# GLA gate, second half: five pairs by seven products, sixteen stored units; PLE preparation, LN1 border and the PLE gate's last units in another order

## The chip, the cores and the metric

The kernel runs on one core of one Trainium2 chip, in one launch. The metric is device time in microseconds. Before the change three runs gave a median of 1651.93 us (1651.26 to 1652.1). One execution was profiled; the trace's rows are from it.

## The reference, cut to what matters

A decoder block over x of 256 tokens by 2048 channels, one layer, all in float32. The part in which the change adds products is the GLA branch's output gate `gr`, one of the column blocks of the combined input projection; two other parts that it reorders are the first layer norm and the per-layer embedding (PLE).

```python
def token_mixers(x, w_in, ...):
    proj = x @ w_in
    gq, gk, gv, gr, glr, fq, fk, fv, ff, ma, mb = jnp.split(proj, offsets, axis=-1)
    ...
    o = gla_chunked(q, k, v, log_a)
    o = o * lax.rsqrt(jnp.mean(o * o, -1, keepdims=True) + RMS_EPS) * gla_norm_g
    o = o.reshape(B, S, GLA_V) * jax.nn.silu(gr)
    y_gla = o @ w_branch_gla
    ...
    merged = jax.nn.sigmoid(ma) * y_gla + jax.nn.sigmoid(mb) * y_fox
    return merged @ w_out

def reference(x, p, ...):
    mix = token_mixers(x, ...)
    x = layer_norm(ALPHA * x + mix, ln1_g, ln1_b)
    ffn = conv_gated_mlp(x, w_gate, w_up, conv_w, conv_b, w_down)
    x = layer_norm(ALPHA * x + ffn, ln2_g, ln2_b)
    return x + jax.nn.sigmoid(x @ w_ple_gate) * (p[0] @ w_ple_proj)
```

## The kernel before

**Units.** All weights come as units of 128 x 2048 float32 (1 MB). `prep()` loads a unit over SP's queue in two halves of 512 KB into `raw` (a ring of five buffers), ACT copies each half to `hi` in the rounded type fp32r (L121), and DVE subtracts to get the remainder `lo` (L241). A product of an activation and a weight is made of three matmuls: activation hi by weight hi, hi by lo, lo by hi. `unit()` gives the next unit to PE's code and prepares up to three ahead.

**Halves.** `s_half` (L818) makes a 2048-deep projection for 1024 output columns: eight pairs of 128-deep blocks, one unit each, into four PSUM quadrants (two of tokens, two of columns) of 128 x 512. A *classic* pair takes 24 matmuls of 512 columns (L844). A pair listed in the half's `_S` table goes by Strassen's seven products instead, 21 matmuls (L852); it needs sums of activations (`x_sums` for the input projection) and four differences of the unit's quarters (L159, DVE). For the pairs listed in a `_T` table the unit is *stored* (`parked`): `park_gen` loads it early, makes its four differences then, and stores 1 MB to `td` in DRAM over POOL's queue (L172); in the half `prep_s` loads a quarter, a half and the 1 MB of `td`, and DVE only makes the remainders (L215), 512 columns and three times 1024. A pair in `_S` but not in `_T` loads the plain unit and makes the differences within the half. After the last Strassen pair `fold` (L862) adds the products' PSUM tiles into the output tile.

**The stored units of the input projection** are those of the two `gv` and two `gr` halves. `park_gen` steps through them in three lots: the first four during FoX, the next four during the GLA's q and k, the rest in the loop of the 20 merge-gate units (`for n in range(PSM1)`), in which PE also makes the chunk scores `pa` (L735) from DVE's `kq` tiles (L718) and DVE makes `x_sums`.

**Order.** A scheduler orders each engine by priorities and modelled readiness, except where the code says `manual_schedule` or `keep_in_program_order`. The LN1 border `end1` (L1310) is under manual schedule on PE. There `turn0(g)` and `turn1(g)` transpose group g of the normalized first or second token half (tile `ptl`, L1212), and `proj(k, t)` makes six matmuls `pp` of the PLE projection (L353). `G` is (1, 0, 3, 2). DVE normalizes the groups by L1196 and L1202 and makes `x1T` from the transposed tiles (L1110, L1227); `put(t)` stores `pp`.

**PLE.** `ple_prep(0)` loads two `praw` halves and `pTr`, and makes `pw` (L1275) and `pTs` (L1280) on ACT and DVE. It is called within `out_proj(0, ...)`, the first half `wo` of the output projection, behind a pair named by its index in the order (0, 1, 3, 4, 5, 2, 6, 7); there pairs 1, 2, 3 and 5 are Strassen, all stored.

**The end.** The last half is `pg`, the PLE gate's second half, with pairs 2, 3 and 4 Strassen. Its last `tail` units are run quadrant by quadrant (L893): for each quadrant all its products, then `ev_g` (L1614), which adds PSUM to `zg`, takes a tanh on ACT, and makes `tho` (L1582) and `res` (L1584) on DVE, which SP stores to the output. The quadrant (1,1) comes last, in two halves of 256 columns (`pg_11b`, `pg_11c`, L909); `pre_g` adds what it had before the tail.

Of the kernel before, what the change touches and what calls it, by code (L numbers as in the profile page):

```python
# [49 lines left out]
GV_ORDER = ((0, 1, 2, 3, 4, 5, 7, 6),) * 2  # L50
GV_S = ((1, 2, 4, 5, 7),) * 2
GV_T = ((1, 2, 5, 7), (1, 2, 5, 7))
GR_T = ((1, 2, 5, 7), (2, 5, 7))
GR_S = ((1, 2, 4, 5, 7), (1, 2, 5, 7))
X_S = (1, 2, 4, 5, 7)
WO_S = ((1, 2, 3, 5), (1, 3, 5))
WO_C = (0, 4, 6, 7)
# [9 lines left out]
PG_S = ((), (2, 3, 4))  # L67
# [11 lines left out]
def tile_block(ctx: ExitStack, tc: tile.TileContext, wu, wfv, wpp, xT_in, x_in, pT_in, wlr,  # L79
# [25 lines left out]
    def s8(shape, dt=F32, name=None):  # L105
        return big.tile(shape, dt, tag="S8", name=name)
# [4 lines left out]
    def t2(name):  # L111
        return sm.tile([P, 512], F32, tag="t2", bufs=6, name=name)

    def mmtile(name):
        return pmm.tile([P, 512], F32, tag="mm", name=name)
# [4 lines left out]
    def copy(o, i, scale=1.0):  # L120
        return nc.scalar.activation(o, i, AF.Copy, bias=0.0, scale=scale)  # L121
# [8 lines left out]
    for _ in range(8):  # L130
# [6 lines left out]
    s_units = {b + nh * len(order[nh]) + i  # L137
               for b, order, sset in ((52, GV_ORDER, GV_S), (68, GV_ORDER, GR_S),
                                      (120, OUT_ORDER, WO_S), (dn0, DN_ORDER, DN_S),
# [4 lines left out]
    parked = {b + nh * len(order[nh]) + order[nh].index(n): None  # L144
              for b, order, tset in ((52, GV_ORDER, GV_T), (68, GV_ORDER, GR_T), (120, OUT_ORDER, WO_T),
                                     (dn0, DN_ORDER, DN_T), (NU - 16, PG_ORDER, PG_T))
# [102 lines left out]
    def unit(ahead=3):  # L249
        u = n_used[0]  # L250
        n_used[0] += 1
        while n_prep[0] < min(NU, u + ahead):
            prep()
        return ready.pop(u)
# [532 lines left out]
    def cell(o, i):  # L787

        return o[:, i, 0:P], o[:, i, P:256]
# [230 lines left out]
    for nh in range(2):  # L1020
        def ev_v(t, c, ps, nh=nh):
            z = vg[2 * nh + c][:, 0, t, :]
            with tc.high_priority(P_STAT):
# [3 lines left out]
               residual=False)  # L1027
# [7 lines left out]
    for nh in range(2):  # L1035
        def ev_r(t, c, ps, nh=nh):
# [3 lines left out]
            if 2 * nh + c == 0:  # L1040
                gate(z, z)

        s_half("gr", nh, GV_ORDER[nh], GR_S[nh], x_cl, x_st, lambda t, g: vg[g][:, 1, t, :], ev_r,
               residual=False)
# [187 lines left out]
    def out_proj(nh, tail, mid, end=None):  # L1232
        def cl(pair, j, t):
            if pair not in WO_C:
                return cell(mS[pair], ((0, 7), (1, 2))[j][t])
            i = WO_C.index(pair)
            a = mC[i // 2][:, i % 2 * 2 + j, :]
            return a[:, t * P:t * P + P], a[:, 256 + t * P:256 + t * P + P]

        def ev(t, c, ps):  # L1240
            zc = z1of(t, 2 * nh + c)
            with tc.high_priority(P_STAT):
                nc.vector.tensor_tensor(zc, zc, ps, ALU.add)
                if tail:
                    nc.vector.bn_stats(st1[t][:, 2 * nh + c, :], zc)

        s_half("wo", nh, OUT_ORDER[nh], WO_S[nh], cl, lambda pair, i: cell(mS[pair], i), z1of, ev,
               tail, mid, end)
# [11 lines left out]
    def load_gain(li, i):  # L1260
        g = s8([P, 2048], name=f"lnb{li}{i}")
        nc.sync.dma_start(g, lng[2 * li + i].broadcast_to([P, 2048]))
        gain[li].append(g)

    def ple_prep(half):

        w = [s8([P, 2048], F32R, name=f"pw{half}{i}") for i in range(2)]
        pt_ = s8([P, 2, 512], F32R, name=f"pTs{half}")
        pTs = [pt_[:, k, :] for k in range(2)]
        for k in range(2):  # L1270
            raw = ring.tile([P, 1024], F32, tag="raw", bufs=5, name=f"praw{half}{k}")
            nc.sync.dma_start(raw, wpp[half, :, k * 1024:k * 1024 + 1024])
            o = slice(k * 1024, k * 1024 + 1024)
            copy(w[0][:, o], raw)
            nc.vector.tensor_tensor(w[1][:, o], raw, w[0][:, o].bitcast(F32), ALU.subtract)  # L1275
        pT = t2("pTr").rearrange("p (k t) -> p k t", t=S)
        nc.sync.dma_start(pT, pT_in)
        for k in range(2):
            copy(pTs[k][:, 0:256], pT[:, k, :])
            nc.vector.tensor_tensor(pTs[k][:, 256:512], pT[:, k, :],  # L1280
                                    pTs[k][:, 0:256].bitcast(F32), ALU.subtract)
        return w, pTs
# [12 lines left out]
    def z1of(t, g):  # L1295
        return z1[t][:, g * 512:g * 512 + 512]
# [11 lines left out]
    pq, first = [], []  # L1308

    def end1(tail_mm):  # L1310

        x1T.extend(s8([P, 4, 512], F32R, name=f"x1T{g}") for g in range(4))
        with tc.manual_schedule(engines={mybir.EngineType.PE}):
            pb = [[[mmtile(f"pp0{t}{c}")] for c in range(2)] for t in range(2)]
            ps, us = [], []

            def proj(k, t):
                o = slice(k * 1024, k * 1024 + 1024)  # L1320
                w, pTs = pq[0]
                x_mm(pb, (w[0][:, o], w[1][:, o]), pTs[k], (t,), k == 0, k == 1)

            def put(t):
                for c in range(2):
                    o = t2("ppo")
                    tc.keep_in_program_order(copy(o, pb[t][c][0]))
                    nc.gpsimd.dma_start(ppd[t, :, c * 512:c * 512 + 512], o)

            kts = [4 * g + i for g in LN_ORDER for i in range(4)]  # L1330

            def phase0(i, part):
                if i == len(us):
                    us.append(unit())
                    ps.append(mmtile(("psg0", "psu0", "psg1")[i]))
                w_phase(ps[i], *us[i], x1T, 0, kts, part)

            def phase1(j):
                for i in range(3):
                    w_phase(ps[i], *us[i], x1T, 1, kts, slice(4 * j, 4 * j + 4))  # L1340

            for c in range(2):
                for i in range(2):
                    tail_mm(0, c, i)
            G = LN_ORDER
            (stat0, norm0, turn0), (stat1, norm1, turn1) = [
                ln_steps(z1of, st1, t, x1T, gain[0], c_g1, c_b1, "l1", P_LN1[t], AFF1[t])
                for t in range(2)]
            stat0()
            for g in G[:2]:  # L1350
                norm0(g)
            for i in range(2):
                tail_mm(1, 0, i)
            tail_mm(1, 1, 0)
            turn0(G[0])
            tail_mm(1, 1, 1)
            turn0(G[1])
            stat1()
            for g in G[2:]:
                norm0(g)  # L1360
            proj(0, 0)
            turn0(G[2])
            proj(1, 0)
            proj(0, 1)
            turn0(G[3])
            put(0)
            for g in G[:2]:
                norm1(g)
            proj(1, 1)
            for i in range(3):  # L1370
                phase0(i, slice(0, 12))
                turn1(G[i])
                if i == 0:
                    put(1)
                    for g in G[2:]:
                        norm1(g)
            for i in range(3):
                phase0(i, slice(12, 16))
            for j in range(4):
                phase1(j)  # L1380
                if j == 1:
                    turn1(G[3])
            first.extend(ps)

    def begin_out():
        for pair in (6, 7):
            turn_pair(pair)
        load_z1()

    out_proj(0, 0, {0: begin_out, 3: lambda: pq.append(ple_prep(0)),  # L1390
                    5: lambda: load_gain(0, 0)})
    out_proj(1, 2, {3: lambda: load_gain(0, 1), 4: stats1}, end1)
    mixers.append(affine(z1of, gain[0], lambda t: nc.gpsimd.dma_start(x1d[t], z1[t]), AFF1))
# [78 lines left out]
    pb, pq = [], []  # L1472
# [122 lines left out]
    def g_sums(pairs):  # L1595
        two = s8([P, 8, 256], F32R, name=f"gS{pairs[0]}")
        for i, pair in enumerate(pairs):
            o = two[:, 4 * i:4 * i + 4]
            a = x2T[pair // 2][:, pair % 2 * 2:pair % 2 * 2 + 2, :].bitcast(F32)
            y = t2("gy").rearrange("p (k t) -> p k t", t=S)  # L1600
            nc.vector.tensor_tensor(y, a[:, :, 0:256], a[:, :, 256:512], ALU.add)
            v = s_sums(y)
            copy(o[:, :, 0:P], v)
            nc.vector.tensor_tensor(o[:, :, P:256], v, o[:, :, 0:P].bitcast(F32), ALU.subtract)
            gS_[pair] = o
# [25 lines left out]
    def mid4():  # L1631
# [4 lines left out]
           begin=begin2, mid=(mid4, 4))  # L1636

    s_half("pg", 1, PG_ORDER[1], PG_S[1], g_cl, g_st, lambda t, g: zg[:, t, g - 2, :], ev_g,
           2, {0: lambda: g_sums(PG_S[1][2:])}, residual=False, fine=pre_g)
    assert n_used[0] == NU, (n_used[0], NU)  # L1640


# [46 lines left out]
def _layout(i):  # L1689
# [8 lines left out]
        [np.stack([_wst(c("fq", 1024)), _wst(c("fk", 1024))], 1).reshape(16, P, 2048), qk.reshape(16, P, 2048), m[:PSM1],  # L1698
         _sst(c("gv", 2048), GV_ORDER, GV_S), _sst(c("gr", 2048), GV_ORDER, GR_S), m[PSM1:]] + br
        + [_sst(i["w_out"][0], OUT_ORDER, WO_S), gu,  # L1700
# [45 lines left out]
```

## Time and profile before

| | us |
|---|---|
| median of three runs | 1651.93 |
| the profiled execution | 1650.91 |
| its span, first to last instruction | 1648.4 |
| PE busy | 1639.4 |
| DVE busy | 1336.8 |
| ACT busy | 903.3 |

In the rows shown below, a row of a timeline gives start and duration in us, the engine, the line, the operation, output and inputs, their shapes and a count; a bracket at its end gives the engine's idle time before it and what ended it. A row of the chain gives start, duration, engine, tile, line and count. A row of the windows gives for a stretch its length and each engine's busy time with the number of instructions, the granted clock of TensorE, the share of DMA time and GB/s. Durations of single matmuls overlap; the spacing of two starts tells how fast they go.

### The profile page before, as it was taken

The page shows a single profiled execution, that of the slowest core. Times are in us where ns is not written, and L with a number is a line of the kernel's source. Part 1 is how long each engine was busy: PE and PEld are TensorE (multiplying, and loading weights), DVE is VectorE, ACT ScalarE, POOL GpSimd, SP SyncE. Part 2 cuts the span into 40 slices and gives each one's busy share as a digit, 9 for nine tenths or more (in the row PEclk, how much of TensorE's full clock was granted, in tenths as well). Part 3 has the DMA queues.
Part 4 walks back from the last instruction along what each step waited for, and adds up shares of the span by engine and source line. Part 5 has one row for each costly group of instructions (what it writes and reads, how often), then busy time and mean ns, then how long its engine had stood idle before and what let it go on. Part 6 is the DMA issues. An engine that isn't in the chain of part 4 may idle for free.

```text
span 1648.4 us, 23392 instructions
## 1 busy us (share of the span) xinstructions
PE 1639.4 (99%) x8429; PEld 1405.7 (85%) x8429; DVE 1336.8 (81%) x1920; ACT 903.3 (55%) x1259; POOL 89.3 (5%) x237
## 2 busy tenths in 40 slices
PE   9999999999999999999999999999999999999998
PEld 8988888888888888888888888888888888888887
DVE  7677789888888767778977888888887778989787
ACT  6755545456656654446574454555455456566554
POOL 0000000000000000000010111110111000000000
PEclk9999999999999999999999999999999999999999
DMA  9777689977878658888855898888776679899574
GB/s 324 279 262 277 227 327 343 345 251 281 292 249 283 228 194 313 304 313 308 303 185 190 315 344 319 298 301 309 277 245 216 212 260 344 299 352 341 172 261 152
DMA packets 111669, 457.35 MB, mean 277 GB/s; under 512 B 12681, under 2 KB 13969, under 8 KB 94657
## 3 DMA queue, kind: packets, MB, share of 16 engines
q1 hardware_dynamic: 103056, 404.47, 69.9%
q0 software_dynamic: 8496, 51.39, 8.0%
q8 instruction: 66, 1.08, 0.3%
q14 instruction: 51, 0.41, 0.1%
HBM read 404.42 MB, written 51.39 MB: 277 GB/s over the span
## 4 chain that ended last, share of the span: by engine, by line
PE 98%; DVE 1%; DMA 0%; ACT 0%; issue 0%; POOL 0%; SPq 0%
PE psm L973 11%; PE dn L841 10%; PE psu L307 10%; PE psg L307 9%; PE psa L973 5%; PE psu L309 5%; PE psg L309 5%; PE dn_p L841 4%; PE wo L841 3%; PE gr L841 3%; PE gv L841 3%; PE pg L353 3%; PE psb L973 3%; PE fv L472 3%; PE pg L841 2%; PE psk L307 2%
## 5 line engine op out<-in xcount | busy, mean ns | idle before, releaser
L241 DVE TENSOR_TENSOR lo<-raw,hi 128x1024 fp32r<-128x1024 f32 x466 | 564.6, 1221 | 165.6 <-ACT hi L121 163.5
L121 ACT ACTIVATE hi<-raw 128x1024 fp32r<-128x1024 f32 x466 | 488.8, 1058 | 350.4 <-DMA raw<-in_wu_dram 66.3
L307 PE MATMUL psu<-x1T,hi 128*128 128x512 f32 x688 | 240.4, 392 | 0.0
L307 PE MATMUL psg<-x1T,hi 128*128 128x512 f32 x672 | 234.9, 392 | 0.0
L309 PE MATMUL psu<-x1T,lo 128*128 128x256 f32 x688 | 192.3, 280 | 0.0
L309 PE MATMUL psg<-x1T,lo 128*128 128x256 f32 x672 | 187.9, 280 | 0.0
L973 PE MATMUL psm<-hi,xT 128*128 128x512 f32 x512 | 163.0, 392 | 0.0
L307 PEld LDWEIGHTS psu<-x1T,hi 128*128 128x128 f32 x688 | 129.2, 188 | 27.6
L307 PEld LDWEIGHTS psg<-x1T,hi 128*128 128x128 f32 x672 | 126.2, 188 | 26.9
L309 PEld LDWEIGHTS psu<-x1T,lo 128*128 128x128 f32 x688 | 130.6, 190 | 0.0
L309 PEld LDWEIGHTS psg<-x1T,lo 128*128 128x128 f32 x672 | 127.6, 190 | 0.1
L121 ACT ACTIVATE hi_b<-raw 128x512 fp32r<-128x512 f32 x102 | 85.4, 841 | 74.4 <-issue 19.1
L215 DVE TENSOR_TENSOR lo_b<-raw,hi_b 128x512 fp32r<-128x512 f32 x102 | 96.7, 954 | 35.1 <-ACT hi_b L121 34.6
L973 PEld LDWEIGHTS psm<-hi,xT 128*128 128x128 f32 x512 | 96.2, 188 | 19.6
L973 PE MATMUL psm<-lo,xT 128*128 128x512 f32 x256 | 99.7, 389 | 0.0
L159 DVE TENSOR_TENSOR td<-td 128x512 f32<-128x512 f32 x144 | 98.7, 685 | 0.6
L841 PE MATMUL dn<-hi,hC 128*128 128x512 f32 x352 | 97.8, 389 | 0.0
L215 DVE TENSOR_TENSOR lo_t<-td,hi_t 128x1024 fp32r<-128x1024 f32 x72 | 85.3, 1219 | 6.3 <-ACT hi_t L121 5.6
L121 ACT ACTIVATE hi_t<-td 128x1024 fp32r<-128x1024 f32 x72 | 75.0, 1055 | 20.4 <-DMA td<-td 6.1
L973 PE MATMUL psa<-hi,oT 128*128 128x512 f32 x256 | 81.1, 392 | 0.0
L841 PEld LDWEIGHTS dn<-hi,hC 128*128 128x128 f32 x352 | 66.0, 188 | 13.7
L121 ACT ACTIVATE hi_t<-raw 128x1024 fp32r<-128x1024 f32 x30 | 31.9, 1062 | 46.1 <-DVE raw L159 39.0
(412 smaller groups left out, 3141.1 us busy)
## 6 DMA issues: line engine op xcount, KB each, us to landing
raw<-in_wu_dram SPq DMA_DIRECT2D x532, 512.0 KB, 5.8
td<-in_wu_dram SPq DMA_DIRECT2D x36, 1024.0 KB, 8.9
td<-td POOLq DMA_DIRECT2D x36, 1024.0 KB, 6.4
td<-td SPq DMA_DIRECT2D x36, 1024.0 KB, 8.2
hS<-sd SPq DMA_DIRECT2D x11, 1024.0 KB, 9.0
raw<-in_wu_dram SPq DMA_DIRECT2D x36, 256.0 KB, 6.3
fvraw<-in_wfv_dram SPq DMA_DIRECT2D x13, 524.0 KB, 7.1
sd<-hs POOLq DMA_DIRECT2D x24, 256.0 KB, 5.8
```

The source lines that it names most:

```text
L121: return nc.scalar.activation(o, i, AF.Copy, bias=0.0, scale=scale)
L159: sub = lambda o, a, b: nc.vector.tensor_tensor(o, a, b, ALU.subtract)
L215: nc.vector.tensor_tensor(lo, src, hi.bitcast(F32), ALU.subtract)
L241: i = nc.vector.tensor_tensor(lo, raw, hi.bitcast(F32), ALU.subtract)
L307: nc.tensor.matmul(ps, lhsT=hi[i // 8 if hoff == 0 else 0][:, w0 % 1024:w0 % 1024 + P], rhs=a[:, kt % 4, :], start=first and i == 0, stop= ...
L309: nc.tensor.matmul(ps[:, 256:512], lhsT=lo[i // 8 if hoff == 0 else 0][:, w0 % 1024:w0 % 1024 + P], rhs=a[:, kt % 4, 0:256], start=False, ...
L353: nc.tensor.matmul(bs[j][:, 0:m], lhsT=x, rhs=v[:, o:o + m], start=first and i == 0, stop=last and i == 2)
L472: nc.tensor.matmul(fbk[t][c][:, 0:n], lhsT=x, rhs=w[:, o:o + n], start=kt == 0 and i == 0, stop=kt == 15 and i == 2)
L841: nc.tensor.matmul(ps[:, e], lhsT=x, rhs=w, start=k == 1, stop=k == total.get(id(ps), 3 * ns))
L973: nc.tensor.matmul(ps[t], lhsT=x, rhs=v, start=first and i == 0 and j == 0, stop=last and i == 3 and j == 2)
```

## The change

The table `GR_S` gets pair 4 for the second half too, and `GR_T` pair 1. So the second half of `gr` has the tables of the first: pairs 1, 2, 4, 5 and 7 by seven products, of which 1, 2, 5 and 7 are stored. The stored units of the projection become 16 instead of 15, in lots of 4, 4 and 8. In `end1` the second six `pp` of the first token half come ahead of the third group's transposes. `ple_prep(0)` is called behind the third pair of the order instead of the fourth. The last half's tail has three units instead of two.

```diff
-GR_T = ((1, 2, 5, 7), (2, 5, 7))
-GR_S = ((1, 2, 4, 5, 7), (1, 2, 5, 7))
+GR_T = ((1, 2, 5, 7), (1, 2, 5, 7))
+GR_S = ((1, 2, 4, 5, 7),) * 2
...
             proj(0, 0)
+            proj(1, 0)
             turn0(G[2])
-            proj(1, 0)
             proj(0, 1)
             turn0(G[3])
...
-    out_proj(0, 0, {0: begin_out, 3: lambda: pq.append(ple_prep(0)),
+    out_proj(0, 0, {0: begin_out, 2: lambda: pq.append(ple_prep(0)),
                     5: lambda: load_gain(0, 0)})
...
     s_half("pg", 1, PG_ORDER[1], PG_S[1], g_cl, g_st, lambda t, g: zg[:, t, g - 2, :], ev_g,
-           2, {0: lambda: g_sums(PG_S[1][2:])}, residual=False, fine=pre_g)
+           3, {0: lambda: g_sums(PG_S[1][2:])}, residual=False, fine=pre_g)
```

On DVE, in the merge-gate stage, the part around the chunk scores that PE makes as `pa_5`; `e` and `kq` are the decayed keys and queries that lead to them, `lo` the remainders of merge-gate units, `at` the masked scores. One piece of the difference:

```order
 L710 TENSOR_TENSOR e<-gb 128x512
-L241 TENSOR_TENSOR lo_0_3628<-raw_0_3624,hi_0_3626 128x1024
-L241 TENSOR_TENSOR lo_1_3634<-raw_1_3630,hi_1_3632 128x1024
+L241 TENSOR_TENSOR lo_0_3635<-raw_0_3631,hi_0_3633 128x1024
 L718 TENSOR_TENSOR kq<-gk,e 128x2x4x32
 L718 TENSOR_TENSOR kq<-gq,e 128x2x4x32
+L241 TENSOR_TENSOR lo_1_3641<-raw_1_3637,hi_1_3639 128x1024
+L740 COPY_PREDICATED at<-mask,pa_5_3655 128x256
```

One of the two remainders has moved behind the two kq; the four differences of the sixteenth stored unit stand about a dozen rows ahead of this piece.

On DVE in the first half of the output projection, before, from the last remainder of the stored unit of pair 2 (the sixth of the order) on; `lo_0` and `lo_1` are the remainders of the classic pair 6 behind it, and `pw` and `pTs` are the PLE preparation:

```order
L215 TENSOR_TENSOR lo_t_7035<-td_7020,hi_t_7034 128x1024
L1275 TENSOR_TENSOR pw_7063<-praw_7065,pw_7062 128x1024
L1275 TENSOR_TENSOR pw_7063<-praw_7069,pw_7062 128x1024
L1280 TENSOR_TENSOR pTs_7064<-pTr,pTs_7064 128x256 x2
L866 TENSOR_TENSOR fold<-fold,wo_p_6950 128x512
L241 TENSOR_TENSOR lo_0_7083<-raw_0_7079,hi_0_7081 128x1024
L865 SCALAR_TENSOR_TENSOR z_6865<-z_6865,fold 128x512
L241 TENSOR_TENSOR lo_1_7089<-raw_1_7085,hi_1_7087 128x1024
```

The same place in the changed kernel:

```order
L1275 TENSOR_TENSOR pw_7031<-praw_7033,pw_7030 128x1024
L1275 TENSOR_TENSOR pw_7031<-praw_7037,pw_7030 128x1024
L1280 TENSOR_TENSOR pTs_7032<-pTr,pTs_7032 128x256 x2
L215 TENSOR_TENSOR lo_b_7054<-raw_0_7047,hi_b_7053 128x512
L215 TENSOR_TENSOR lo_b_7058<-raw_1_7048,hi_b_7057 128x1024
L215 TENSOR_TENSOR lo_t_7062<-td_7051,hi_t_7061 128x1024
L215 TENSOR_TENSOR lo_t_7066<-td_7051,hi_t_7065 128x1024
L241 TENSOR_TENSOR lo_0_7097<-raw_0_7093,hi_0_7095 128x1024
L241 TENSOR_TENSOR lo_1_7103<-raw_1_7099,hi_1_7101 128x1024
L866 TENSOR_TENSOR fold<-fold,wo_p_6964 128x512
```

The PLE preparation has moved ahead of the stored unit's four remainders, and both remainders of the classic pair ahead of the fold.

On DVE at the very end, before; `zg` is the gate's sum, `pg_10` the quadrant (1,0), `pg_11b` and `pg_11c` the two halves of the last quadrant:

```order
L1617 TENSOR_TENSOR zg<-zg,pg_10_15199 128x512
L1623 TENSOR_TENSOR zg<-zg,pg_11b 128x256
L1582 SCALAR_TENSOR_TENSOR tho<-tho,ppk_14793 128x512
L1584 SCALAR_TENSOR_TENSOR res<-tho,z_14003 128x512
L1623 TENSOR_TENSOR zg<-zg,pg_11c 128x256
```

And in the changed kernel:

```order
L1617 TENSOR_TENSOR zg<-zg,pg_10_15213 128x512
L1582 SCALAR_TENSOR_TENSOR tho<-tho,ppk_14807 128x512
L1623 TENSOR_TENSOR zg<-zg,pg_11b 128x256
L1584 SCALAR_TENSOR_TENSOR res<-tho,z_14017 128x512
L1582 SCALAR_TENSOR_TENSOR tho<-tho,ppk_14807 128x256
L1584 SCALAR_TENSOR_TENSOR res<-tho,z_14017 128x256
L1623 TENSOR_TENSOR zg<-zg,pg_11c 128x256
```

The `tho` and `res` of the first half of the last quadrant now stand ahead of the addition of its second half.

## The prediction

> **What bounds the kernel now.** I read the page first, then the list of PE's waits, then the windows by stage, and last the rows around the four places that the change touches.
>
> ```profile
> PE 1639.4 (99%) x8429; PEld 1405.7 (85%) x8429; DVE 1336.8 (81%) x1920; ACT 903.3 (55%) x1259; POOL 89.3 (5%) x237
> engine line waited for: us in total, times, longest us
> PE warm_ps L131 <- DVE warm L128: 1.2, 1, 1.2
> PE ptl L1212 <- DVE z L1202: 1.0, 1, 1.0
> PE fv L472 <- ACT fvhi L121: 0.6, 1, 0.6
> PE wo L841 <- DVE lo L241: 0.6, 1, 0.6
> core 0: us, PE busy (x) PEld busy (x) DVE busy (x) ACT busy (x) POOL busy (x), PEclk, DMA share, GB/s
> 330.00:350.00 20.00, 20.00 (x98) 16.86 (x98) 18.07 (x34) 11.35 (x18) 0.53 (x1) 1.00 0.75 256
> 350.00:368.30 18.30, 18.30 (x89) 15.33 (x89) 15.41 (x31) 9.06 (x15) 0.00 (x0) 1.00 0.72 225
> 448.70:489.00 40.30, 40.30 (x179) 33.33 (x178) 35.24 (x39) 24.71 (x27) 0.00 (x0) 1.00 0.81 291
> 489.00:529.70 40.70, 40.70 (x181) 33.67 (x180) 34.84 (x39) 25.72 (x28) 0.00 (x0) 1.00 0.73 258
> 1626.00:1648.40 22.40, 17.09 (x87) 14.46 (x85) 15.88 (x24) 4.76 (x8) 0.00 (x0) 0.94 0.17 63
> ```
>
> PE is busy 1639.4 of 1648.4 us; the span before the last stage has only four waits, 3.4 us in all, of which two (ptl and wo, 1.6 us) lie where the change works. What is left is the end: in the last window PE has 17.09 of 22.40 us, so some 5 us stand behind its last matmul. So there are three ways to gain here: fewer matmuls, the two stalls, and what follows PE's last matmul. Nothing else can move the end, unless something that is now hidden comes to stand before PE. In 330 to 350 us DVE works 18.07 of 20.00 us, so it is the engine to watch. The clock is full in all these windows but the last, whose 0.94 includes the idle tail.
>
> **The GLA gate's second half: three matmuls fewer.** Pair 4 goes from 24 matmuls to seven products of three.
>
> ```profile
> 448.66 5.44 PE gr L841 x24
> 1640.22 1.45 PE pg_11b L909 x12
> ```
>
> One classic pair of the first half takes 5.44 us for 24, which is 226.7 ns a matmul; twelve of 256 columns take 1.45 us, 120.8 ns each. The term is 3 x 226.7 ns = -0.68 us, all of it on PE's chain. The Trainium skill ("TensorE: Matmul & The Clock Gate", section "Back-to-back issue gap") gives a warm spacing of N/2.4 + 2.5 ns, an estimate of 216 ns at 512 columns and 109 at 256. By that rule this term is an estimated -0.65 us; the trace's 226.7 and 120.8 ns do not agree with it, and they decide.
>
> What feeds it: in this half pair 1 is now stored, pair 4 not. Each unit that is not stored costs DVE four differences inside the half; they move from pair 1 to pair 4, so their number there is the same. New are the remainders: 512 + 3 x 1024 columns in place of 2 x 1024.
>
> ```profile
> L159 DVE TENSOR_TENSOR td<-td 128x512 f32<-128x512 f32 x144 | 98.7, 685 | 0.6
> 358.99 0.69 DVE L215 TENSOR_TENSOR lo_b<-raw,hi_b 128x512 fp32r<-128x512 f32 x1
> 1621.73 1.22 DVE L215 TENSOR_TENSOR lo_t<-td,hi_t 128x1024 fp32r<-128x1024 f32 x1
> ```
>
> That is 0.69 + 1.22 = 1.9 us more on DVE, 34.84 + 1.9 = 36.7 of 40 us. The first half has the same five pairs and the same stored four already and runs 40.30 of 40.30 us without a PE wait, on a DVE of 35.24. I therefore cost it at nothing; what hides it is PE's 40 us, and without that cover it is 1.9 us.
>
> **The sixteenth stored unit.** Its differences move into the merge-gate stage: four of L159, 4 x 685 ns = 2.74 us by the mean, on DVE, plus a load and a store of 1 MB each. The DMA share there is 0.75 and 0.72 at 256 and 225 GB/s against 291 in the row of the first gate half, so 2 MB have room in 38 us. DVE has 20.00 - 18.07 + 18.30 - 15.41 = 4.8 us free, and the 2.74 fit. What can be hurt is PE's small score products, which wait for the kq tiles of DVE.
>
> ```profile
> 348.93 1.05 PE L735 MATMUL pa<-kq 128*128 128x128 f32 x8
> 357.99 1.24 PE L735 MATMUL pa<-kq 128*128 128x128 f32 x8
> 358.05 0.42 DVE L718 TENSOR_TENSOR kq<-gq,e 128x256 f32<-128x256 f32 x1
> 356.57 1.22 DVE L241 TENSOR_TENSOR lo<-raw,hi 128x1024 fp32r<-128x1024 f32 x1 [0.18 <-ACT hi L121]
> ```
>
> Today the second kq ends at 358.47 while its products began at 357.99; the eight products ahead of that took 1.05 us, these 1.24, so PE is held some 0.19 us. The changed order puts one of the two 1.22 us remainders ahead of kq behind it, which gives back 1.22 while the differences add 2.74, with 0.18 us of idle in between. The bounds are -0.19 (kq in time) and 2.74 - 1.22 + 0.19 = +1.7 us (all of it late). DVE's work before it is done ahead of need with idle to spare, so I take the near end, **-0.19**.
>
> **The LN1 border.** Here PE follows the written order strictly.
>
> ```profile
> 825.58 1.64 PE L353 MATMUL pp<-pw,pTs 128*128 128x512 f32 x6
> 828.27 0.63 PE L1212 MATMUL ptl<-ident,z 128*128 128x128 f32 x4 [1.05 <-DVE z L1202]
> 827.39 0.73 DVE L1202 SCALAR_TENSOR_TENSOR z<-z,mv,lnb 128x512 f32<-128x512 f32 x1
> 830.35 0.68 DVE L1110 TENSOR_TENSOR x1T<-ptl,x1T 128x512 fp32r<-128x512 f32 x1
> ```
>
> Six pp begin at 825.58 and hold PE to 825.58 + 6 x 0.2267 = 826.94. The transposes of the third group then stand until 828.27 because DVE's L1202 ends at 828.12. By the spacing the hole is 1.33 us (the view shows 1.05, as it counts a matmul's modelled end). With proj(1,0) first, twelve pp reach to 825.58 + 2.72 = 828.30, and z is there at 828.27: the hole is gone even if L1202 comes no sooner. What could be late next is the fourth group's transposes and then the gate's first matmuls, which stand behind another twelve pp as before and so come 1.33 earlier; the third group's x1T is done at 830.35 + 0.68 = 831.03, twelve pp behind 828.30 reach to 831.02 already, and PE turns to that group only behind the first two, so it lies ahead. Term **-1.33 us**, bounds -1.33 and 0.
>
> **The PLE preparation, one pair earlier.**
>
> ```profile
> 764.15 2.35 DVE L215 TENSOR_TENSOR lo_t<-td,hi_t 128x1024 fp32r<-128x1024 f32 x2
> 766.42 1.22 DVE L1275 TENSOR_TENSOR pw<-praw,pw 128x1024 fp32r<-128x1024 f32 x1
> 768.93 1.23 DVE L1275 TENSOR_TENSOR pw<-praw,pw 128x1024 fp32r<-128x1024 f32 x1 [1.29 <-ACT pw L121]
> 770.07 0.75 DVE L1280 TENSOR_TENSOR pTs<-pTr,pTs 128x256 fp32r<-128x256 f32 x2
> 771.58 1.22 DVE L241 TENSOR_TENSOR lo<-raw,hi 128x1024 fp32r<-128x1024 f32 x1
> 771.23 1.07 PE L841 MATMUL wo<-hi,mC 128*128 128x512 f32 x4
> 772.86 0.73 PE L841 MATMUL wo<-lo,mC 128*128 128x512 f32 x2 [0.56 <-DVE lo L241]
> ```
>
> PE's four hi products would end at 771.23 + 4 x 0.2267 = 772.14; the remainder they are followed by is made from 771.58 and PE goes on at 772.86, a hole of 0.72 us (0.56 in the view). In front of it on DVE stand pw twice, pTs and a fold, with 1.29 us of waiting for ACT inside. After the change pw and pTs come before the remainders of the stored pair ahead, and both remainders of the classic pair before the fold. So 2 x 1.22 + 0.75 us of work and the wait are gone from the place of the hole, more than the 0.72 that is needed.
>
> In return the two praw and the pTr loads (1.25 MB) stand on SP's queue ahead of that stored pair's three loads, with four copies on ACT. The pair's 21 products end at 771.23, so they begin at 766.47, and the tenth, the first to use the row at 764.15, at 768.51; that remainder is done at 764.15 + 1.22 = 765.37, 3.1 us ahead.
>
> ```profile
> 740.60:821.00 80.40, 79.84 (x356) 65.88 (x356) 70.63 (x82) 46.11 (x51) 0.00 (x0) 1.00 0.87 314
> raw<-in_wu_dram SPq DMA_DIRECT2D x532, 512.0 KB, 5.8
> ```
>
> At this stage's 314 GB/s the 1.25 MB (1.31 million bytes) take 4.2 us: 1.1 us too late if the pair's loads wait for all of them, early enough if they share the engines and each lands about its 5.8 us behind its issue. Term **-0.72**, bounds -0.72 and -0.72 + 1.1 = +0.4.
>
> **The tail of three units in the PLE gate.**
>
> ```profile
> 1625.94 14.28 PE pg L841 x63
> 1631.79 1.22 DVE L241 TENSOR_TENSOR lo<-raw,hi 128x1024 fp32r<-128x1024 f32 x1
> 1642.81 0.69 DVE L1584 SCALAR_TENSOR_TENSOR res<-tho,z 128x512 f32<-128x512 f32 x1
> 1643.42 0.41 DVE L1623 TENSOR_TENSOR zg<-zg,pg_11c 128x256 f32<-128x256 f32 x1
> 1645.00 0.42 DVE L1584 SCALAR_TENSOR_TENSOR res<-tho,z 128x256 f32<-128x256 f32 x1
> ```
>
> PE: from pair 5 on there were 60 matmuls of 512 and 24 of 256 columns, 60 x 226.7 + 24 x 120.8 = 16.50 us; now 54 and 36, 16.59: +0.09. By the spacings of the Trainium skill's page named above, an estimate of this difference is +0.02. But the end hangs on DVE: PE's last product ends at 1640.22 + 2 x 1.45 = 1643.12, and DVE adds its half at 1643.42 only, since res of the quadrant before stands ahead. With eighteen products in each half the quadrant (1,0) is done at 1625.94 + 57 x 0.2267 = 1638.86 and its chain through DVE is finished before PE's end, now 1643.21. Then DVE takes the last half at about 1643.24, and behind it stand the tanh, one tho and one res as before; but the tho and res of the half ahead (0.34 + 0.35 us) no longer hold them, which leaves the last res at about 1645.02 instead of 1645.42. Term **-0.40**. What could hold PE are the remainders of the last two units. The last is done at 1631.79 + 1.22 = 1633.01. Pair 5 begins at 1625.94 + 3 x 0.2267 = 1626.62, and in the built order that remainder is first read by the 37th matmul, at 1634.8: 1.8 us to spare, since the products of three quadrants are interleaved. If this cover is gone it is the fourth rival.
>
> **The sum**: -0.68 - 0.19 - 1.33 - 0.72 - 0.40 = -3.32 us. The profiled execution took 1650.91 us, so it would take 1647.6; it lies 1.0 us under the median of the runs shown, so the median goes from 1651.93 to **1648.6 us**.
>
> **The rivals.**
>
> *The holes move on.* PE's two waits (0.72 + 1.33) end, but what stood behind them is late in its turn: the PLE loads delay the stored pair by as much, the fourth group's transposes find z or a PSUM bank unready. For it: in the rows of both holes DVE works without a pause of its own but the one behind ACT, so all that stands behind the hole is late with it. Against: the pair has 3.1 us in hand, and the third z is ready at the very time the new order asks for it. Then -3.32 + 2.05 = -1.27 us, 1650.7.
>
> *DVE becomes the bound (slower).* The place is 330 to 368 us and the second gate half. If DVE's 4.8 us idle there are waits for ACT and PE that cannot be filled, the 2.74 us of differences and the 1.9 us of remainders come out on PE's path whole: -3.32 + 0.19 + 2.74 + 1.9 = +1.5 us, 1653.4. It decides the sign from 3.3 us of lateness on. For it: 18.07 of 20.00 in the first window, and PE's score products already held there by kq. Against: PE has no wait of a view in either stage, and the first gate half carries the added load already.
>
> *Only the score products are late*, by the upper bound above: -3.32 + 0.19 + 1.7 = -1.4 us, 1650.5.
>
> *The tail of three holds PE.* Were the products run in the written order, quadrant by quadrant, the seventeenth would need the remainder of 1633.01 at 1626.62 + 16 x 0.2267 = 1630.25: +2.8 us, 1651.4. The built order says otherwise, but it decides only if the loads of the last unit come as in the trace.
>
> That the change doesn't do what it says is ruled out by the built order: 21 products for pair 4, twelve pp before the third transposes, 36 matmuls of 256 columns at the end.
>
> **How the numbers follow.** 0.2% of 1651.93 is 3.3 us, about what a measurement of this kernel can tell from no change; the forecast of -3.32 lies on it. Forecast 0.68, with a range of its own of 1647.6 to 1649.4 (upper end: the waits as the view shows them, 1.05 and 0.56, and no gain from kq, -2.7 and so 1649.2; lower end: one us more than the sum, as the profiled execution lies one under the median); 0.47 of it I put on the side of over 0.2%, as the holes by spacing are what PE gets back, 0.21 within. Holes move on 0.14 (within), score products or tail late 0.07 (within), DVE the bound 0.11: 1653.4 is within 0.2% itself, but a DVE that is bound would bring a hole back too (+2.05, 1655.4), so I put 0.08 of it over and 0.03 within. So faster 0.47, same 0.45, slower 0.08. The range: the forecast's own leaves out too much, so it reaches over the rivals at 1650.5 to 1651.4, and somewhat further below: 1647.2 to 1651.6.
>
> **What would show it.** In the list of PE's waits, ptl behind z and wo behind lo are gone, and nothing new of over 0.3 us stands there. The second gate half reads 40.0 us in place of 40.7, PE full. In the border, pp x12 starts at once behind the second group's transposes, and the first psg follows 1.3 us sooner. At the end pg_11b and pg_11c take 2.2 us each, and the last res ends about 1.8 us behind PE in place of 2.3. Wrong it would be by a wait of PE at pa behind kq, at gr or wo_p behind lo_t or td, or at pg behind lo; or if PE's spacing left 226.7 ns, as the tiles of the last two thirds lie elsewhere in SBUF, for which no row speaks.

## The result, and the profile after

The changed kernel takes 1648.59 us (median of 21 runs, 1648.25 to 1655.85), the kernel before, measured beside it, 1651.44 us (21 runs, 1650.91 to 1653.14): 2.85 us less. The ratio is 0.9985 with a 95% interval of 0.9980 to 0.9991, so it is faster, by less than 0.2%. The predicted 1648.6 us is met, the predicted difference of 3.32 us is not: the kernel before was shown by three runs half a microsecond higher than by 21, and, as the rows below show, one of the five terms came out with the other sign.

The page's row of engines and the list of PE's waits, of the changed kernel (line; what it waited for; us in total, times, longest):

```profile
PE 1639.6 (100%) x8432; PEld 1405.6 (85%) x8432; DVE 1339.6 (81%) x1926; ACT 904.5 (55%) x1261; POOL 89.5 (5%) x238
PE warm_ps L131 <- DVE warm L128: 1.2, 1, 1.2
PE wo_p L841 <- ACT hi_t L121: 0.5, 2, 0.3
```

The span fell from 1648.4 to 1646.5 us in the profiled executions. The waits of ptl behind z and of wo behind lo are gone, and in the place of the second stands a new one, wo_p behind ACT's hi_t. (The wait of fv, 0.6 us in the profile before, belongs to the first loads and comes and goes with the execution.)

Where the time went is read best from PE's own progress: the start of a matmul that both kernels have, after minus before. The list gives this lag at seven marks, each the start of the first matmul into the named tile, from the two traces; pg_p is its last matmul, and the end is the last res:

```
mark                     before     after      lag    step
smp  (after the fv part)   50.74     51.11    +0.37   +0.37  first loads
gv   (gv begins)          368.08    368.24    +0.16   -0.21  score products
go   (behind gr)          544.46    543.93    -0.53   -0.69  second gate half
ptl  (LN1 border begins)  823.34    823.03    -0.31   +0.22  output projection
psu  (behind the border)  835.10    833.55    -1.55   -1.24  LN1 border
pg_p (last)              1625.55   1624.01    -1.54   +0.01  MLP, LN2, PLE gate
last res ends            1645.42   1643.45    -1.97   -0.43  the tail
```

Four of the five terms stand there at their size: -0.21 for -0.19, -0.69 for -0.68, -1.24 for -1.33, -0.43 for -0.40. The fifth has the wrong sign: +0.22 in place of -0.72.

The windows of the changed kernel (length; busy time of PE, weight loads, DVE, ACT, POOL; clock, DMA share, GB/s), for the merge-gate stage and the second gate half:

```profile
330.00:350.00 20.00, 20.00 (x98) 16.82 (x97) 19.51 (x36) 10.51 (x17) 0.53 (x1) 1.00 0.83 284
350.00:368.30 18.30, 18.30 (x93) 15.47 (x91) 16.39 (x34) 9.89 (x16) 0.53 (x1) 1.00 0.71 240
489.00:529.00 40.00, 40.00 (x178) 33.06 (x178) 36.74 (x41) 26.73 (x29) 0.00 (x0) 1.00 0.79 284
```

DVE has grown from 33.48 to 35.90 us in the first two and from 34.84 to 36.74 in the gate half, as counted, and PE is full in all three. The score products on PE's and DVE's timelines (start, duration, operation, count):

```profile
358.36 1.05 PE L735 MATMUL pa<-kq 128*128 128x128 f32 x8
357.89 0.42 DVE L718 TENSOR_TENSOR kq<-gq,e 128x256 f32<-128x256 f32 x1
358.31 1.23 DVE L241 TENSOR_TENSOR lo<-raw,hi 128x1024 fp32r<-128x1024 f32 x1
```

kq ends at 358.31, 0.05 us ahead of PE, and the eight products take 1.05 us, not 1.24; the second remainder stands behind kq, as the built order said. The border, on the chain of the changed kernel (start, duration, engine and tile, count):

```profile
825.08 0.44 PE ptl L1212 x4
825.51 2.75 PE pp L353 x12
828.27 0.44 PE ptl L1212 x4
828.70 1.39 PE pp L353 x6
...
831.92 1.44 PE psg L322 x12
```

No piece of another engine stands between them: PE goes through. And the end, on the same chain:

```profile
1639.47 2.17 PE pg_11c L909 x18
1641.64 0.03 issue
1641.67 0.43 DVE zg L1623
...
1642.12 0.42 ACT tho L1581
...
1642.57 0.44 DVE tho L1582
...
1643.03 0.42 DVE res L1584
```

DVE takes the last half 0.03 us behind PE, and the last res ends at 1643.45, 1.81 us behind PE's last product (2.30 before).

What went wrong in the output projection is on PE's, ACT's and the loads' rows there (a bracket gives the idle time before and what ended it):

```profile
768.42 0.73 PE L841 MATMUL wo_p<-hi_t,mS 128*128 128x512 f32 x2 [0.27 <-ACT hi_t L121]
769.37 0.50 PE L841 MATMUL wo_p<-hi_t,mS 128*128 128x512 f32 x1 [0.21 <-ACT hi_t L121]
766.83 0.60 ACT L121 ACTIVATE fold<-wo_p 128x512 f32<-128x512 f32 x1 [4.38 <-PE wo_p L841]
767.32 1.99 ACT L121 ACTIVATE hi_t<-td 128x1024 fp32r<-128x1024 f32 x2
755.50 0.42 SPq L196 DMA_DIRECT2D td<-td  x1
DMA to landing us min/median/max: 6.9/6.9/6.9
```

The stored pair's td is issued at 755.50 and lands 6.9 us later, at 762.4, in time. But ACT idles 4.38 us until 766.83: its next instruction is the fold's first copy, which waits for a product of the same pair on PE, and hi_t stands behind it until 767.32. PE asks for hi_t at about 768.0 and gets it at 768.42, the second at 769.37. By the spacing of the matmuls the two holes are 0.93 us, for the 0.72 us that went; the difference, 0.21, is the step of the lag.

### The profile page after: what moved, and what is told of

It is laid out like the page before. It is cut to its first block, busy times and chain, and to the rows that moved or that the text cites. A ratio compares the mean times of both kernels' runs of the same rounds, so it can differ in the third digit from the quotient of the medians.

```text
span 1646.5 us, 23416 instructions
## 1 busy us (share of the span) xinstructions
PE 1639.6 (100%) x8432; PEld 1405.6 (85%) x8432; DVE 1339.6 (81%) x1926; ACT 904.5 (55%) x1261; POOL 89.5 (5%) x238
## 4 chain that ended last, share of the span: by engine, by line
PE 98%; DMA 1%; DVE 0%; ACT 0%; issue 0%; POOL 0%; SPq 0%; DVEq 0%; ACTq 0%; POOLq 0%
PE psm L973 11%; PE dn L841 10%; PE psu L307 10%; PE psg L307 9%; PE psa L973 5%; PE psu L309 5%; PE psg L309 5%; PE dn_p L841 4%; PE gv L841 3%; PE gr L841 3%; PE wo L841 3%; PE pg L353 3%; PE psb L973 3%; PE fv L472 2%; PE psk L307 2%; PE psq L307 2%
```

## The experiments

**Each of the four edits alone**, on the kernel before.

```diff
 # e1_gr: the two tables
+GR_T = ((1, 2, 5, 7), (1, 2, 5, 7))
+GR_S = ((1, 2, 4, 5, 7),) * 2
 # e2_ln1
             proj(0, 0)
+            proj(1, 0)
             turn0(G[2])
-            proj(1, 0)
 # e3_ple
-    out_proj(0, 0, {0: begin_out, 3: lambda: pq.append(ple_prep(0)),
+    out_proj(0, 0, {0: begin_out, 2: lambda: pq.append(ple_prep(0)),
 # e4_tail
-           2, {0: lambda: g_sums(PG_S[1][2:])}, residual=False, fine=pre_g)
+           3, {0: lambda: g_sums(PG_S[1][2:])}, residual=False, fine=pre_g)
```

> Only the two tables change: five pairs by seven products in both halves of gr, sixteen stored units. If the terms add up, PE gains 0.2 us at the score products pa in the merge-gate stage and 0.68 us in the second gate half, 0.9 us by the end, with the two waits of before (ptl behind z 1.0, wo behind lo 0.6) still listed. If DVE becomes the bound there, PE shows a new wait at pa, gr or gr_p and the kernel is slower than before by up to 3.9 us.

> Only proj(1,0) ahead of the third group's transposes. If the hole vanishes whole, the first up matmuls psu come 1.3 us sooner against the last wo matmul than before, and ptl behind z is gone from the list of waits. If the wait moves on to the fourth group's transposes or to psg, the gain is under 0.7 us and another wait of PE stands in the list.

> Only the PLE preparation one pair earlier. By the prediction's term PE gains 0.7 us in the first half of the output projection. By what the changed kernel's trace shows, the wait of wo behind lo is replaced by waits of wo_p behind ACT's hi_t of the stored pair, and the half is no shorter: 0.2 us longer. If those waits belong to the other parts of the change, they are not here.

> Only the tail of three units. If the term is right, the last matmul comes 0.1 us later against pair 5's start than before, and the last res ends 1.8 us behind PE's last product in place of 2.3, 0.4 us sooner in all. If a remainder holds PE in the tail, pg behind lo stands in the list of waits and the end is up to 2.4 us later.

Measured against the kernel before (1651.59 us): 1650.05 us for the tables (ratio 0.9991, 0.9982 to 1.0001), 1649.97 for the border (0.9990, 0.9980 to 0.9999), 1649.72 for the PLE preparation (0.9989, 0.9980 to 0.9999), 1650.63 for the tail (0.9994, 0.9985 to 1.0004). The intervals reach some 1.6 us to each side, too wide for terms of this size. The four differences of the medians add up to 6.0 us, where all four edits together gain 2.85: they cannot simply be added. The steps of PE's lag from one profile each, at the same marks, tell more:

```
step               e1_gr   e2_ln1   e3_ple   e4_tail   all four
first loads        +0.50    +0.36    +0.57     +0.62      +0.37
score products     -0.21     0.00     0.00      0.00      -0.21
second gate half   -0.68     0.00    +1.25      0.00      -0.69
output projection  -0.01    +0.04    +0.21      0.00      +0.22
LN1 border         +0.01    -1.19    -1.24     -0.02      -1.24
MLP to PLE gate    +0.11    -0.01    +0.39     +0.40      +0.01
```

Each gain sits where its edit is. Three things stand out. The first loads are 0.36 to 0.62 us later in these four and in the changed kernel than in the profile before; in the later runs the same step lies between -0.21 and +0.93, so it belongs to the execution and not to an edit. The PLE move alone costs 0.21 us in the output projection, so its new wait is its own; the step is +0.20 to +0.22 in all six profiles that have the move as it stands, and 0.00 to +0.04 in the four other kernels without it. And it closes the border's hole too, in which it changes no line. (The +1.25 is one wait of gr_p behind DVE's lo_t in that one execution, which took 1651.55 us where the other nine took 1649.35 to 1650.47; the +0.4 in the MLP is, in the tail's and in the PLE move's profile, one stop of psg at 947.9 and 948.0 us, where the chain runs through DVE and ACT to a remainder lo.) The list of waits of the PLE move alone:

```profile
PE warm_ps L131 <- DVE warm L128: 1.2, 1, 1.2
PE gr_p L841 <- DVE lo_t L215: 0.8, 1, 0.8
...
PE wo_p L841 <- ACT hi_t L121: 0.5, 2, 0.3
```

No ptl behind z is in it (the row left out is the first loads', fv). For the tail alone the chain's end:

```profile
1642.01 2.17 PE pg_11c L909 x18
1644.18 0.02 issue
1644.20 0.43 DVE zg L1623
...
1645.57 0.42 DVE res L1584
```

Its last res ends at 1645.99, 1.81 us behind PE, and 19.44 us behind the last pg_p in place of 19.87: the term of 0.40, at 0.43.

**The changed kernel with the fold's copy behind hi_t on ACT.** What ACT and PE compute is the same; only the place of one copy in ACT's queue is fixed.

```diff
+            made[u] = copy(hi, src)
...
-            copy(u, p1)
+            if nh == 0 and nm == "wo":
+                with tc.issue_after(made[n_used[0] - 1].ins):
+                    copy(u, p1)
+            else:
+                copy(u, p1)
```

> The changed kernel, with the fold's first copy on ACT queued behind the stored pair's two hi_t copies. If that in-order copy is what replaced the prediction's term of 0.72 us, the two waits of wo_p behind ACT hi_t are gone and the first half of the output projection is 0.9 us shorter than in the changed kernel. If the td load is late in itself, because the PLE loads stand ahead of it on SP's queue, the waits stay, with the DMA as their cause.

1647.34 us against 1651.32 (0.9976, 0.9966 to 0.9985). The output projection is 1.07 us shorter than in the changed kernel (0.88 ahead of it at ptl, where it was 0.19 behind at the projection's start), and no wait of wo_p is listed. So the in-order copy on ACT was the whole loss, and the PLE loads ahead on SP's queue cost nothing. Against the kernel before, the projection is now 0.85 us shorter: with the copy out of the way the PLE move gives the 0.72 us that the prediction put on it, and a little more. The profiled execution of this run, 1654.59 us, lost 7 us later in the MLP (the other ten executions took 1646.56 to 1647.95 us); only its rows ahead of that are used, and the last section comes back to it.

**The changed kernel without the PLE move.**

```diff
-    out_proj(0, 0, {0: begin_out, 2: lambda: pq.append(ple_prep(0)),
+    out_proj(0, 0, {0: begin_out, 3: lambda: pq.append(ple_prep(0)),
```

> The changed kernel with the PLE preparation back behind the fourth pair. By the prediction's term it is 0.7 us slower than the changed kernel. By its trace, in which the move cost 0.2 us, it is 0.2 us faster there, with wo behind lo back in the list of waits.

1648.57 us (0.9982, 0.9973 to 0.9991), the same as the changed kernel. By the lag the output projection is 0.21 us shorter than in the changed kernel, with wo behind lo (0.6) back in the list. So within the changed kernel the prediction's 0.7 us for this edit is ruled out, in sign too; the medians alone could not tell 0.2 us from nothing.

**The changed kernel without the new order at the border.**

```diff
             proj(0, 0)
-            proj(1, 0)
             turn0(G[2])
+            proj(1, 0)
```

> The changed kernel with proj(1,0) back behind the third transposes. If the order of proj alone closes the border's hole, the hole of 1.2 us is back and ptl waits for z. The run with the PLE move alone had no such wait, so the rival is that DVE's order at the border, which the PLE move also changes, closes it too: then the time is that of the changed kernel within 0.3 us.

1648.77 us (0.9983, 0.9974 to 0.9992): the same again, and from ptl to psu the lag moves by 0.04 us only. The chain shows how:

```profile
824.79 0.44 PE ptl L1212 x4
825.23 1.40 PE pp L353 x6
826.62 0.44 PE ptl L1212 x4
827.06 2.77 PE pp L353 x12
```

The third transposes start at 826.62, right behind six pp, without waiting. The L1202 that they need must therefore be one that was done by then, the one that ends at 826.27; the next one, also shown, ends at 827.53 only:

```profile
825.53 0.75 DVE L1202 SCALAR_TENSOR_TENSOR z<-z,mv,lnb 128x512 f32<-128x512 f32 x1
826.19 0.69 DVE L1245 BATCH_NORM_STATS2 st<-z 128x6 f32<-128x512 f32 x1
826.79 0.74 DVE L1202 SCALAR_TENSOR_TENSOR z<-z,mv,lnb 128x512 f32<-128x512 f32 x1
```

In the kernel before PE went on only behind the later one of the pair (827.39 to 828.12). So, by the waits, DVE has the group that PE needs first as the earlier of the two once the PLE work before them is moved; the same stands in the profile of the PLE move alone. Why the scheduler turns them round is not shown. So the hole of 1.2 us is closed twice over, and each of the two edits is worth nothing there once the other is made.

**The tail in the written order.** PE's tail of the changed kernel put under manual schedule, so that it runs quadrant by quadrant.

```diff
+            with tc.manual_schedule(engines={mybir.EngineType.PE}):
                 for t, c in ((0, 0), (0, 1), (1, 0)):
                     for i in range(tail):
                         tail_mm(t, c, i)
...
                 for b, ps in enumerate(halves):
```

> The changed kernel with PE's tail in the written order, quadrant by quadrant, not interleaved. If the remainders of the last two units are as late as the prediction's fourth rival says, pg waits behind lo for 2.8 us and the end is that much later than in the changed kernel. If the trace's remainders come sooner than thought, the waits are under 1 us.

1652.18 us, 3.6 more than the changed kernel and no longer to be told from the kernel before (1.0006, 0.9997 to 1.0015). PE's lag against the changed kernel grows by 3.1 us from the last pg_p to the last product (the profiled execution, 1651.36 us, was the quickest of the ten). From its list of waits:

```profile
PE pg L841 <- DVE lo L241: 2.2, 3, 0.8
```

These are three waits, 2.2 us as the view counts them. A tail of three units is a gain only because the scheduler interleaves the quadrants.

**More work on DVE behind the sixteenth stored unit.** Subtractions into a tile that nothing reads are added, four in one kernel and eight in another.

```diff
         nc.gpsimd.dma_start(td[i], w)
+        if i == 15:
+            for _ in range(8):
+                d = t2("dum")
+                nc.vector.tensor_tensor(d, w[:, 0:512], w[:, 512:1024], ALU.subtract)
```

> The changed kernel with four more subtractions of 128x512 on DVE (2.7 us) right behind the sixteenth stored unit's differences, into a tile that nothing reads. If DVE has the 2 to 3 us of slack there that the prediction counted on, no wait of PE appears between 330 and 370 us and PE reaches gv as in the changed kernel. If DVE is already the bound, PE waits at pa or psm for up to 2.7 us.

> The same with eight more (5.5 us). DVE's idle time in 330 to 368 us of the changed kernel is 0.5 + 1.9 = 2.4 us, so by that count PE should be held for up to 3 us; if the remainders' lead of some us counts as slack too, PE is held for less than 1 us.

Each kernel was run once. The mark is gr, not gv, since the first gv product stands ahead of some of the score products in these two. With four, PE is at gr as in the changed kernel (the lag between the two moves by 0.02 us) and no wait of this stage is listed; the execution took 1648.35 us. With eight it took 1649.92 us, PE is held for 1.84 us up to gr, and three waits stand in this stage's list:

```profile
PE gv L845 <- DVE lo_b L219: 0.4, 1, 0.4
PE psm L977 <- DVE lo L245: 0.3, 1, 0.3
PE pa L739 <- DVE kq L722: 0.2, 1, 0.2
```

(Line numbers are four higher there.) So DVE has room for about 5.5 - 1.8 = 3.7 us more in that place, beyond the 2.7 us that the sixteenth unit took: more than its 2.4 us of idle there. The likely reason is that the remainders run some us ahead of PE and can fall back: with four subtractions DVE's busy time from 368.3 to 448.7 us is 72.69 us in place of 70.44, so most of the 2.7 us comes out there, under the two gv halves, without a wait.

**Both: the copy behind hi_t, and the border's order as before.**

> The kernel with the fold's copy queued behind hi_t on ACT, and proj(1,0) back behind the third transposes. If the PLE move's effect on DVE's order at the border closes the hole there by itself, no ptl waits for z and the time is that of the mended kernel, 1.2 us under the changed one. If the mended order loses that side effect, the hole of 1.2 us is back and the time is that of the changed kernel.

1647.18 us against 1651.35 (0.9974, 0.9964 to 0.9984). Its whole list of PE's waits, and ACT at the place in question:

```profile
PE warm_ps L131 <- DVE warm L128: 1.2, 1, 1.2
763.63 2.01 ACT L121 ACTIVATE hi_t<-td 128x1024 fp32r<-128x1024 f32 x2 [1.41 <-DMA td<-td]
765.55 1.05 ACT L121 ACTIVATE hi<-raw 128x1024 fp32r<-128x1024 f32 x1
766.55 0.60 ACT L121 ACTIVATE fold<-wo_p 128x512 f32<-128x512 f32 x1
```

hi_t is made at 763.63, as soon as td is there, 3.7 us sooner than in the changed kernel (3.4 when the 0.27 us by which this execution was ahead is taken off), and the fold's copy fits in later without holding anybody. With 1.2 to 1.4 us less than the changed kernel, the two mended kernels are the fastest seen; between them the new border order makes no difference.

## Why the prediction was right, and where it was not

**Three matmuls fewer** (-0.68): shown, -0.68 alone and -0.69 in the whole. DVE's added 1.9 us lay beside PE as the first gate half had promised.

**The score products** (-0.19): shown, -0.21 in every kernel with the sixteenth unit whose DVE work is otherwise as in the change. The near end of the bounds was the right one, though kq came only 0.05 us ahead of PE.

**The border** (-1.33): the hole went, for 1.2 us; the count by spacing was 0.1 too high, for a reason that is not shown. But it isn't owed to the reordered products alone. That the hole would be closed twice was not seen, so the sum held a gain that the PLE move would have brought by itself.

**The PLE preparation** (-0.72): the step that failed. The old hole did go, as DVE's order had promised, but a new one of 0.93 us came 3 us earlier, net +0.22. The prediction looked for it on SP's queue and gave a bound of +0.4 for loads that come late; the loads came in time. It counted "four copies on ACT" as the only thing that is new there, and never looked at what else had changed places in ACT's order: the fold's copy, which waits for PE, now stood ahead of the pair's hi_t. In the profile before, the two stood the other way round on ACT:

```profile
762.88 2.14 ACT L121 ACTIVATE hi_t<-td 128x1024 fp32r<-128x1024 f32 x2
...
767.35 0.60 ACT L121 ACTIVATE fold<-wo_p 128x512 f32<-128x512 f32 x1 [1.39 <-PE wo_p L841]
```

There hi_t was made 4.5 us ahead of the fold's copy. The Trainium skill says of ACT that its queue is strictly first in, first out ("Perfetto Trace Analysis", section "Tensor Engine Instruction (MATMUL, LD_WEIGHTS)"); the 4.38 us of idle on ACT with td already landed agree. The rival "the holes move on" was right for this one of the two, by another cause than it named.

**The tail** (-0.40): shown at -0.43, with DVE's queue at the end as the cause. The fourth rival's price of 2.8 us was right too: 3.1 us in the written order.

**DVE as the bound**: excluded in the merge-gate stage, with some 3.7 us to spare by one execution. In the second gate half DVE is busy 36.74 of 40.00 us and PE waits for nothing; how much more it could take there was not tried.

**The total.** The terms by the lag make -0.21 - 0.69 + 0.22 - 1.24 - 0.43 = -2.35 us, where -3.32 was forecast; of the 0.97 between them 0.94 are the PLE term. The measured difference is 2.85. Of the remaining 0.50 us, 0.43 lie outside the span: time minus span has a median of 2.42 us in the runs of the kernel before and of 1.99 in those of the changed one. The predicted time came out exact because this, and a kernel before that is 0.5 us faster in 21 runs than in three, made up for the failed term. The mechanism was right at four places of five, at one of them not alone; that the time agrees to 0.01 us is luck. The range says little here: 1647.2 to 1651.6 reaches past the 1651.44 us of the kernel before. And the outcome with the largest chance, faster by over 0.2% (0.47), did not come; it needed the PLE term, and the two kernels with ACT's copy put behind hi_t are at 0.24% and 0.26%.

## What to carry to other kernels

When an edit moves work through a scheduler, compare the built order on every engine at that place, the quiet ones too: an engine at 55% that works strictly in order can hold a critical tile behind one copy that waits for someone else. Gains of edits made apart don't add where two of them close the same hole; leave one out at a time before crediting either. And where the effects are smaller than the runs' spread, the lag of one engine's matching instructions between two traces shows each of them to some hundredths of a microsecond.

## What the runs showed of the hardware that was not expected

The time outside the span is not the same for all these kernels: 2.42 us (median) for the kernel before and 2.38 for the one with the border edit alone, 1.88 to 2.06 for the nine others that were run nine times or more, the change's among them. Some runs of the first two were at 1.97 to 2.06 as well. Nothing in the traces shows where it lies, and it was not settled; it differs between kernels that are alike but for the order of some instructions.

The first loads alone make the start of PE's main work vary by 1.15 us between profiled executions (first matmul behind the fv part at 50.53 to 51.68 us), in kernels that are the same up to there; the differences arise in the first 12 us.

The spacing of PE's products can differ without a wait and at the same clock. In the profile of 1654.59 us (the copy behind hi_t) the products of 512 columns in the MLP's gate and up stage, from 944 to 1324 us, start 235.8 ns apart; in each of the twelve other profiles they start 229.6 ns apart. The granted clock reads 1.00 in both and no wait of PE is listed there, so the spacing alone makes the 7 us. It belongs to that execution and not to the kernel, whose other ten executions ended some 7 us sooner; its cause was not found. One execution of the changed kernel, at 1655.85 us, is as far off, but was not profiled.
